# A hybrid decoder layer on one core: four Strassen pieces instead of three in each SwiGLU down product, and two of four weight sums per piece made by adding DMAs

## The chip, the core and the metric

The kernel runs on one NeuronCore of a Trainium2 chip. Five engines work side by side on their own instruction queues: TensorE (PE, matrix products; PEld is its loading of stationary operands), VectorE (DVE), ScalarE (ACT), GpSimd (POOL) and SyncE (SP, which here only issues DMAs). Data lies in DRAM, is brought by DMA into SBUF (128 partitions), and products accumulate in PSUM banks of 128 x 512 float32. The metric is device microseconds of one execution; lower is better. Before the change three runs took 733.73, 734.62 and 734.84 us.

## What is computed

One decoder layer on 256 tokens of width 1024, float32 throughout: a SwiGLU block with half a residual, a mixer (an SSD branch beside differential attention, merged by gates), and a second SwiGLU block, each between RMS norms. The change touches the down product of both SwiGLU blocks only:

```python
def swiglu(x, w_gate, w_up, w_down):
    return (jax.nn.silu(x @ w_gate) * (x @ w_up)) @ w_down
...
h = h + 0.5 * rmsnorm(swiglu(rmsnorm(h, ffn1_pre_g[l]), ffn1_w_gate[l], ffn1_w_up[l], ffn1_w_down[l]),
                      ffn1_post_g[l])
...
h = h + 0.5 * rmsnorm(swiglu(rmsnorm(h, ffn2_pre_g[l]), ffn2_w_gate[l], ffn2_w_up[l], ffn2_w_down[l]),
                      ffn2_post_g[l])
```

The down weight is 2816 x 1024, so the down product is (256 x 2816) times (2816 x 1024).

## The kernel before

**Float32 by three products.** Every float32 operand x is split into hi, x rounded to the PE's fast 32-bit format, and lo = x - hi. A product is hi*hi + lo*hi + hi*lo: three matmuls where one would do. For weights the split is made while the kernel runs: ScalarE casts a piece of weight to hi (L259 for plain chunks, L130 in `Quad.split`), VectorE subtracts to get lo (L262, L135). So each weight passes through ScalarE and VectorE once, in instructions of 128 x 1024.

**Chunks and buffers.** The list `chunks` holds every weight tile in the order of use, 1 MB each. `load_to` (L231 to L239) issues their loads on SP's queue into `RAW_BUFS` = 3 buffers named raw, so that a new load starts when an older chunk has been split. The split parts, the weight sums (wt), the activations of the down product (gh and gl, a hi and a lo tile for every 512 of the 2816 rows) and the larger sums of activations are all 4 KB tiles of one pool, k4, with `K4_BUFS` = 29 slots. A tile takes a slot at its first write and gives it back after its last reader; an instruction whose tile finds no free slot waits, and so does what is behind it on its engine.

**The down product.** It is cut along its 2816 rows in eleven chunks of 256 rows (numbers 0 to 10). `DOWN` (L49) is the plan: p is one plain chunk, q1 is a piece of two chunks (2 and 3), q2 is 4 and 5, q3 is 6 and 7. A plain chunk needs 24 matmuls of 128 x 512. A piece is a 2 x 2 by 2 x 2 block product, done by Winograd's form of Strassen with seven products in place of eight: 42 matmuls in place of 48. Its weights lie in two raw buffers: the first holds quarters 0 and 1 (upper left and right), the second quarters 2 and 3 (lower left and right). Products 1, 2 and 3 use plain quarters 0, 2 and 3; products 5, 6, 7 and 4 use sums, which VectorE makes in `sum_of` (L122), one sum ahead of its use. `FIRST` and `LAST` (L50) are the orders of the seven products in a piece, `LAST` for the last piece. The sums of the activations are made once per piece in `sums_of` (L667 on), when the piece's chunks of activations are ready.

**Order.** Pieces and the plain chunks between them are done in `mm_quads` over both 128-token blocks at once. The last three plain chunks (`TAIL` = 3) are done in `mm_n` block by block, so that the norm of block 0 runs while the PE works on block 1; between the two parts `combine` (L723 to L729) adds the Strassen products up on VectorE, ordered behind the lo part of the last chunk. `take` (L287) hands out the next split weight and first splits ahead by `AHEAD` = 3 chunks, where a product of a piece counts a quarter of a chunk. `give_back` frees a raw buffer as soon as its two quarters have had their last use, and issues the next load into it. Engines other than the PE follow in this part the order that the scheduler gave them when the kernel was built.

**GpSimd** does little: its queue holds the loads of the norm's gains (`load_gain`, L587) and small work.

Of the kernel before, what the change touches and what calls it, by code (L numbers as in the profile page):

```python
# [26 lines left out]
P = 128  # L27
T = 256
# [17 lines left out]
QK_US = 2.4  # L46
GATE_US = 1.75
SSD_US = 1.55
DOWN = {"f1": "q1 p q2 p q3 ppp", "f2": "q1 p q2 p q3 ppp"}  # L49
FIRST, LAST = (1, 2, 3, 5, 7, 6, 4), (1, 6, 7, 2, 5, 3, 4)  # L50
BREAK, STOP = object(), object()

# [2 lines left out]
def tile_hybrid_layer(ctx: ExitStack, tc: tile.TileContext, x, ffn1_pre_g, ffn1_w_gate, ffn1_w_up,  # L55
# [37 lines left out]
    class Quad:  # L93

        PLAIN = {1: 0, 2: 2, 3: 3}
        SUMS = {5: (1, 0), 6: (3, 5), 7: (3, 1), 4: (2, 6)}

        def __init__(self, i, products):  # L100
            self.i, self.sums, self.products = i, {}, products
            self.uses = [[p for p in products if p in (1, 5)], [p for p in products if p in (5, 7)],
                         [p for p in products if p in (2, 4)], [p for p in products if p in (3, 6, 7)]]

        def quarter(self, n, p):

            self.uses[n].remove(p)
            return raws[self.i + n // 2][:, :, (n % 2) * 512:(n % 2 + 1) * 512]

        def give_back(self):  # L110
            for j in range(2):
# [4 lines left out]
        def sum_of(self, p):  # L116

            if p not in self.sums:
                n, m = self.SUMS[p]
                m = self.sum_of(m) if p in (6, 4) else self.quarter(m, p)  # L120
                t = k4([P, 2, 512], f"wt{self.i}{p}")
                nc.vector.tensor_sub(t, self.quarter(n, p), m)  # L122
                self.sums[p] = t
            return self.sums[p]

        def split(self, p):
            load_to(self.i + 2)
            hi = k4([P, 2, 512], f"wqh{self.i}{p}", F32R)
            src = self.quarter(self.PLAIN[p], p) if p in self.PLAIN else self.sum_of(p)
            nc.scalar.copy(hi, src)  # L130
            for later in self.products[self.products.index(p) + 1:][:1]:
                if later in self.SUMS:
                    self.sum_of(later)
            lo = k4([P, 2, 512], f"wql{self.i}{p}", F32R)
            nc.vector.tensor_sub(lo, src, hi.bitcast(F32))  # L135
            self.give_back()
            return lambda kt: hi[:, kt, :], lambda kt: lo[:, kt, :]

    chunks, units = [], []

    def chunk(src, shape):
        units.append((len(chunks), None))
# [11 lines left out]
    def quad(w, k0, products):  # L156

        n = len(units)
        for k in (k0, k0 + 2 * P):
            n_chunk(w, k)  # L160
        del units[n:]
        q = Quad(len(chunks) - 2, products)
        units.extend((q, p) for p in products)


# [65 lines left out]
    def load_to(n):  # L231
        while len(raws) < min(n, len(chunks)):
            i = len(raws)
            src, shape = chunks[i]
            r = sb.tile(shape, F32, tag="raw", name=f"raw{i}", bufs=RAW_BUFS)
            nj = shape[1] // 4 if i == 0 else shape[1] // 2 if i < 4 else shape[1]
            for j in range(0, shape[1], nj):
                nc.sync.dma_start(r[:, j:j + nj, :], src[:, j:j + nj, :])
            raws.append(r)  # L239

    def split_steps(ahead=True):

# [344 lines left out]
        nc.gpsimd.dma_start(pg, v[0].partition_broadcast(P))  # L587
        return pg

    def mm_n(acc, acts, ready, turned, begun=lambda: None, pairs=None, begin=True, taken_all=lambda: None, norms=None,  # L590
             half=lambda b, q: None, quarters=(), tail=None):


# [8 lines left out]
        def one(i, w, parts, late=True, others=True, cs=slice(0, 512), to=None):  # L602
# [3 lines left out]
            for kt in range(2):  # L606
                ah, al = acts[2 * pairs[i] + kt]
                for b, qs in parts:
                    ts = slice(b * P, (b + 1) * P)
                    for x_, w_ in ((ah, wh), (al, wh), (ah, wl)):  # L610
                        if not (late if kt == 1 and w_ is wl else others):
                            continue
                        for q in qs:
                            nc.tensor.matmul(acc[b][q][:, cs] if to is None else to, x_[:, ts],  # L614
                                             w_(kt)[:, halves[q]][:, cs],
                                             start=to is not None and kt == 0 and x_ is ah and w_ is wh or
                                             begin and i == 0 and kt == 0 and x_ is ah and w_ is wh,
                                             stop=i == n - 1 and kt == 1 and w_ is wl)
                if i == 0:
                    begun()  # L620
# [46 lines left out]
    def sums_of(g, even, odd):  # L667
# [3 lines left out]
        v = k4([P, 4, 2, P], f"sv{g}")  # L671
        hi, lo = ((k3 if g < 3 else k4)([P, 3, 2, P], f"s{n}{g}", F32R) for n in "hl")
        more = k2([P, 2, 2, P], f"s4{g}", F32R)
        nc.vector.tensor_tensor(v[:, 0], even[:, :, bs[1]], odd[:, :, bs[1]], ALU.add)
        nc.vector.tensor_sub(v[:, 2], even[:, :, bs[0]], even[:, :, bs[1]])
        nc.vector.tensor_sub(v[:, 1], v[:, 0], even[:, :, bs[0]])
        nc.vector.tensor_sub(v[:, 3], odd[:, :, bs[0]], v[:, 1])
        split(hi, lo, v[:, 0:3])
        split(more[:, 0], more[:, 1], v[:, 3])
        return ([hi[:, i] for i in range(3)] + [more[:, 0]], [lo[:, i] for i in range(3)] + [more[:, 1]])  # L680
# [1 line left out]
    def mm_quads(acts, sums, tag):  # L682
# [40 lines left out]
        def combine():  # L723
# [1 line left out]
            m = add(u2, bank[6], p1)  # L725
            tc.add_manual_dep(m.ins, last_wlo[0].name, order, reason="behind the last chunk's weights")
            add(u3, bank[7], u2)
            add(u4, bank[5], u2)
            add(c4, bank[5], u3)  # L729

        return acc, [[p1, u4], [u3, c4]], combine, [j for kind, j in down[tag][n_quads:]]

# [75 lines left out]
    def ffn(post_v, tag, ready, turned, then, products):  # L808
# [64 lines left out]
        def done(b):  # L873
            norm_end(norms[b], b, 4.0, tag)
            ready(b)

        mm_n(acc, gu, done, turned, pairs=pairs, begin=False,
             taken_all=combine, norms=norms, half=half, quarters=quarters, tail=tail)


# [687 lines left out]
```

## Time and profile before

| | us |
|---|---|
| three runs | 733.73, 734.62, 734.84 |
| span of the profiled execution, first to last instruction | 732.0 |
| median of the runs less that span | 2.6 |
| PE busy | 724.0 (4025 matmuls) |
| VectorE busy | 609.2 |
| ScalarE busy | 475.3 |
| GpSimd busy | 37.0 |
| DMA, mean over the span | 188 GB/s, 137.92 MB |

The page gives the time that each engine had an instruction in work. The time of the profiled execution outside its span isn't on the page; the runs are 1.7 to 2.8 us longer than the span. Views with windows give the same busy times for a stretch of the span, and the timeline lists instructions with start, duration, engine, line and tiles; a bracket behind a row is the idle time before it and what ended it. The first SwiGLU's down product lies at about 130 to 190 us, the second's at 666 to 725 us, and both run the same code.

### The profile page before, as it was taken

How to read it: one execution, taken by the hardware profiler on the slowest of the kernel's cores; microseconds unless marked ns; L12 is line 12 of the kernel's file. 1: busy time of each engine (PE TensorE's matmuls, PEld its weight loads, DVE VectorE, ACT ScalarE, POOL GpSimd, SP SyncE). 2: the span in 40 equal slices, each digit the busy share in tenths (PEclk: the TensorE clock that was granted, in tenths of full speed). 3: DMA queues.
4: the chain of work that ended last, by engine and by line, in shares of the span. 5: the costliest groups of instructions: out<-in, count | busy, mean ns of one | idle time of the engine just before them, and what ended most of it. 6: DMA issues, size and time to landing. Idle time of an engine off the chain costs nothing.

```text
span 732.0 us, 10570 instructions
## 1 busy us (share of the span) xinstructions
PE 724.0 (99%) x4025; PEld 618.4 (84%) x4025; DVE 609.2 (83%) x948; ACT 475.3 (65%) x815; POOL 37.0 (5%) x66
## 2 busy tenths in 40 slices
PE   9999999999999999999999999999999999999996
PEld 7888888888878889999888888888888888888885
DVE  6978787999979999877996997784784878779995
ACT  6656566656867676869965577772663657566562
POOL 2800000000200000000000000000010000000000
PEclk9999999999999999999999999999999999999999
DMA  8874645467673647666564664475471664654541
GB/s 290 241 247 157 225 146 203 173 210 279 182 228 118 201 146 250 187 192 207 159 221 146 215 209 147 140 246 187 129 238 35 231 195 153 227 205 145 185 185 57
DMA packets 94210, 137.92 MB, mean 188 GB/s; under 512 B 2684, under 2 KB 68304, under 8 KB 94160
## 3 DMA queue, kind: packets, MB, share of 16 engines
q1 hardware_dynamic: 91488, 129.51, 53.1%
q0 software_dynamic: 2368, 7.22, 3.2%
q8 instruction: 31, 0.51, 0.3%
q10 hardware_dynamic: 304, 0.53, 0.2%
q14 instruction: 19, 0.16, 0.1%
HBM read 136.17 MB, written 1.08 MB: 188 GB/s over the span
## 4 chain that ended last, share of the span: by engine, by line
PE 99%; DVE 0%; ACT 0%; DVEq 0%; issue 0%; ACTq 0%
PE pup_f L326 9%; PE pg_f L326 9%; PE pws L345 6%; PE pgt L345 6%; PE acc_f1p L692 5%; PE acc_f2p L692 5%; PE pxs L326 4%; PE pg_f L325 4%; PE pup_f L325 4%; PE pn_f L355 3%; PE acc_mx L614 3%; PE pn_mx L345 3%; PE pn_f L345 3%; PE pwd L345 3%; PE acc_f1p L614 2%; PE acc_f2p L614 2%
## 5 line engine op out<-in xcount | busy, mean ns | idle before, releaser
L262 DVE TENSOR_TENSOR wlo<-raw,whi 128x1024 fp32r<-128x1024 f32 (+1 forms) x222 | 262.2, 1209 | 19.5 <-ACT whi L259 18.3
L259 ACT CAST whi<-raw 128x1024 fp32r<-128x1024 f32 (+1 forms) x221 | 222.8, 1043 | 12.8 <-PE psc L1255 2.5
L326 PE MATMUL pup_f<-u_f,whi 128*128 128x512 f32 x288 | 101.5, 396 | 0.0
L326 PE MATMUL pg_f<-u_f,whi 128*128 128x512 f32 x288 | 101.3, 396 | 0.0
L325 PE MATMUL pg_f<-u_f,wlo 128*128 128x256 f32 x252 | 70.6, 280 | 0.0
L325 PE MATMUL pup_f<-u_f,wlo 128*128 128x256 f32 x252 | 70.3, 279 | 0.0
L326 PEld LDWEIGHTS pup_f<-u_f,whi 128*128 128x128 f32 x288 | 52.9, 188 | 9.9
L326 PEld LDWEIGHTS pg_f<-u_f,whi 128*128 128x128 f32 x288 | 52.8, 188 | 9.7
L325 PEld LDWEIGHTS pg_f<-u_f,wlo 128*128 128x128 f32 x252 | 47.5, 189 | 1.7
L325 PEld LDWEIGHTS pup_f<-u_f,wlo 128*128 128x128 f32 x252 | 47.5, 189 | 1.6
L326 PE MATMUL pxs<-u_mx,whi 128*128 128x512 f32 x128 | 44.6, 397 | 0.0
L130 ACT CAST wqh<-wt 128x1024 fp32r<-128x1024 f32 x24 | 25.3, 1054 | 23.3 <-DVE wt L122 22.1
L330 ACT COPY su_f<-pup_f 128x256 f32<-128x256 f32 x36 | 13.4, 372 | 37.5 <-PE pup_f L326 37.4
L331 DVE TENSOR_TENSOR su_f<-pup_f,su_f 128x256 f32<-128x256 f32 x36 | 15.1, 421 | 25.0 <-ACT su_f L330 24.9
L345 PE MATMUL pgt<-whi,u_mx 128*128 128x512 f32 x128 | 33.1, 393 | 0.0
L311 PE MATMUL pz<-u_mx,whi 128*128 128x256 f32 x128 | 31.8, 285 | 0.0
L312 PE MATMUL pz<-u_mx,whi 128*128 128x256 f32 x128 | 31.4, 283 | 0.0
L325 PE MATMUL pxs<-u_mx,wlo 128*128 128x256 f32 x112 | 31.2, 279 | 0.0
L135 DVE TENSOR_TENSOR wql<-wt,wqh 128x1024 fp32r<-128x1024 f32 x24 | 29.2, 1218 | 0.2
L345 PEld LDWEIGHTS pgt<-whi,u_mx 128*128 128x128 f32 x128 | 23.6, 188 | 5.3 <-issue 0.7
L326 PEld LDWEIGHTS pxs<-u_mx,whi 128*128 128x128 f32 x128 | 23.2, 188 | 4.2
L301 ACT CAST gh_f<-sg_f 128x512 fp32r<-128x512 f32 x18 | 11.2, 620 | 23.0 <-DVE sg_f L848 23.0
(415 smaller groups left out, 1699.1 us busy)
## 6 DMA issues: line engine op xcount, KB each, us to landing
raw<-in_w_in_dram SPq DMA_DIRECT2D x40, 1024.0 KB, 5.2
raw<-in_ffn_w_down_dram SPq DMA_DIRECT2D x22, 1024.0 KB, 4.9
raw<-in_ffn_w_gate_dram SPq DMA_DIRECT2D x20, 1024.0 KB, 5.2
raw<-in_ffn_w_up_dram SPq DMA_DIRECT2D x20, 1024.0 KB, 5.2
raw<-in_ssd_w_branch_dram SPq DMA_DIRECT2D x8, 1024.0 KB, 4.9
acb<-acd POOLq DMA_DIRECT2D x8, 512.0 KB, 5.0
raw<-in_da_w_branch_dram SPq DMA_DIRECT2D x4, 1024.0 KB, 4.9
raw<-in_w_out_dram SPq DMA_DIRECT2D x4, 1024.0 KB, 4.9
```

Source lines behind the costliest of these rows:

```text
L130: nc.scalar.copy(hi, src)
L135: nc.vector.tensor_sub(lo, src, hi.bitcast(F32))
L259: behind(copy(hi[:, js, :], r[:, q * nj + j:q * nj + j + n, :]), "cast")
L262: m = nc.vector.tensor_sub(lo[:, js, :], r[:, q * nj + j:q * nj + j + n, :], hi[:, js, :].bitcast(F32))
L311: nc.tensor.matmul(acc[m], wh(j)[:, cs], ah(k0 + j), start=first and j == ks[0], stop=False)
L312: nc.tensor.matmul(acc[m], wh(j)[:, cs], al(k0 + j), start=False, stop=False)
L325: nc.tensor.matmul(acc[:, :T], wl(j)[:, cs], ah(j), start=False, stop=False)
L326: nc.tensor.matmul(acc, wh(j)[:, cs], ahl(j), start=j == 0, stop=j == KD - 1)
L345: nc.tensor.matmul(acc, a(k0 + j), b(j), start=first and i == 0, stop=last and i == 11)
L355: nc.tensor.matmul(accs[b], x_(k0 + j), w_(j), start=first and j == 0 and w_ is wh and x_ is acts[b][0], stop=last and j == 3 and w_ is wl)
L614: nc.tensor.matmul(acc[b][q][:, cs] if to is None else to, x_[:, ts], w_(kt)[:, halves[q]][:, cs], start=to is not None and kt == 0 and x_ ...
L692: nc.tensor.matmul(bank[p], x_, w_, start=p not in begun, stop=last and p in (1, 5, 6, 7))
```

## The change

`DOWN` becomes "q1 q2 q3 q4 ppp" for both blocks: chunks 8 and 9 become a fourth piece, the pieces stand in a row, and the three plain chunks 0, 1 and 10 come last. For each piece two of the four weight sums aren't made by VectorE any more. `added`, called when the piece's first raw buffer is loaded, lets GpSimd's queue add quarter 0 from DRAM into quarter 1 in the raw buffer (product 5's sum, with accumulating DMA), takes a k4 tile, loads quarter 1 into it on SP's queue, and adds quarter 3 to it with a second accumulating DMA on GpSimd's queue (product 7's sum). The sums then are additions with the opposite sign for some, so signs turn in `sum_of`, `sums_of` and `combine`. Quarter 0 is now used by products 1 and 6, quarter 1 by 5, quarter 2 by 2 and 4, quarter 3 by 3. `begin` of `mm_n` becomes a function, since the bank of the fourth block of the result now gets its first product only in the tail.

```diff
--- before.py
+++ after.py
@@ -46,7 +46,7 @@
 QK_US = 2.4
 GATE_US = 1.75
 SSD_US = 1.55
-DOWN = {"f1": "q1 p q2 p q3 ppp", "f2": "q1 p q2 p q3 ppp"}
+DOWN = {"f1": "q1 q2 q3 q4 ppp", "f2": "q1 q2 q3 q4 ppp"}
 FIRST, LAST = (1, 2, 3, 5, 7, 6, 4), (1, 6, 7, 2, 5, 3, 4)
 BREAK, STOP = object(), object()
 
@@ -94,18 +94,27 @@
 
 
 
-        PLAIN = {1: 0, 2: 2, 3: 3}
-        SUMS = {5: (1, 0), 6: (3, 5), 7: (3, 1), 4: (2, 6)}
-
-        def __init__(self, i, products):
-            self.i, self.sums, self.products = i, {}, products
-            self.uses = [[p for p in products if p in (1, 5)], [p for p in products if p in (5, 7)],
-                         [p for p in products if p in (2, 4)], [p for p in products if p in (3, 6, 7)]]
+        PLAIN = {1: 0, 5: 1, 2: 2, 3: 3}
+
+        def __init__(self, i, w, k0, products):
+            self.i, self.w, self.k0, self.sums, self.products = i, w, k0, {}, products
+            self.uses = [[p for p in products if p in (1, 6)], [5], [p for p in products if p in (2, 4)], [3]]
 
         def quarter(self, n, p):
 
             self.uses[n].remove(p)
             return raws[self.i + n // 2][:, :, (n % 2) * 512:(n % 2 + 1) * 512]
+
+        def of_dram(self, k, c):
+            return self.w[self.k0 + k * T:self.k0 + (k + 1) * T, c * 512:(c + 1) * 512].rearrange(
+                "(j p) c -> p j c", p=P)
+
+        def added(self):
+
+            nc.gpsimd.dma_start(raws[self.i][:, :, 512:], self.of_dram(0, 0), accum_op=ALU.add)
+            t = self.sums[7] = k4([P, 2, 512], f"wt{self.i}7")
+            nc.sync.dma_start(t, self.of_dram(0, 1))
+            nc.gpsimd.dma_start(t, self.of_dram(1, 1), accum_op=ALU.add)
 
         def give_back(self):
             for j in range(2):
@@ -116,10 +125,10 @@
         def sum_of(self, p):
 
             if p not in self.sums:
-                n, m = self.SUMS[p]
-                m = self.sum_of(m) if p in (6, 4) else self.quarter(m, p)
+                n, m = {6: (0, 7), 4: (2, 6)}[p]
+                m = self.sum_of(m)
                 t = k4([P, 2, 512], f"wt{self.i}{p}")
-                nc.vector.tensor_sub(t, self.quarter(n, p), m)
+                nc.vector.tensor_tensor(t, self.quarter(n, p), m, ALU.add)
                 self.sums[p] = t
             return self.sums[p]
 
@@ -129,7 +138,7 @@
             src = self.quarter(self.PLAIN[p], p) if p in self.PLAIN else self.sum_of(p)
             nc.scalar.copy(hi, src)
             for later in self.products[self.products.index(p) + 1:][:1]:
-                if later in self.SUMS:
+                if later in (4, 6):
                     self.sum_of(later)
             lo = k4([P, 2, 512], f"wql{self.i}{p}", F32R)
             nc.vector.tensor_sub(lo, src, hi.bitcast(F32))
@@ -138,7 +147,7 @@
 
 
 
-    chunks, units = [], []
+    chunks, units, quads = [], [], {}
 
     def chunk(src, shape):
         units.append((len(chunks), None))
@@ -159,7 +168,7 @@
         for k in (k0, k0 + 2 * P):
             n_chunk(w, k)
         del units[n:]
-        q = Quad(len(chunks) - 2, products)
+        q = quads[len(chunks) - 2] = Quad(len(chunks) - 2, w, k0, products)
         units.extend((q, p) for p in products)
 
 
@@ -237,6 +246,8 @@
             for j in range(0, shape[1], nj):
                 nc.sync.dma_start(r[:, j:j + nj, :], src[:, j:j + nj, :])
             raws.append(r)
+            if i in quads:
+                quads[i].added()
 
     def split_steps(ahead=True):
 
@@ -587,7 +598,7 @@
         nc.gpsimd.dma_start(pg, v[0].partition_broadcast(P))
         return pg
 
-    def mm_n(acc, acts, ready, turned, begun=lambda: None, pairs=None, begin=True, taken_all=lambda: None, norms=None,
+    def mm_n(acc, acts, ready, turned, begun=lambda: None, pairs=None, begin=lambda b, q: True, taken_all=lambda: None, norms=None,
              half=lambda b, q: None, quarters=(), tail=None):
 
 
@@ -614,7 +625,7 @@
                             nc.tensor.matmul(acc[b][q][:, cs] if to is None else to, x_[:, ts],
                                              w_(kt)[:, halves[q]][:, cs],
                                              start=to is not None and kt == 0 and x_ is ah and w_ is wh or
-                                             begin and i == 0 and kt == 0 and x_ is ah and w_ is wh,
+                                             begin(b, q) and i == 0 and kt == 0 and x_ is ah and w_ is wh,
                                              stop=i == n - 1 and kt == 1 and w_ is wl)
                 if i == 0:
                     begun()
@@ -671,10 +682,10 @@
         v = k4([P, 4, 2, P], f"sv{g}")
         hi, lo = ((k3 if g < 3 else k4)([P, 3, 2, P], f"s{n}{g}", F32R) for n in "hl")
         more = k2([P, 2, 2, P], f"s4{g}", F32R)
-        nc.vector.tensor_tensor(v[:, 0], even[:, :, bs[1]], odd[:, :, bs[1]], ALU.add)
+        nc.vector.tensor_sub(v[:, 0], even[:, :, bs[1]], odd[:, :, bs[1]])
         nc.vector.tensor_sub(v[:, 2], even[:, :, bs[0]], even[:, :, bs[1]])
         nc.vector.tensor_sub(v[:, 1], v[:, 0], even[:, :, bs[0]])
-        nc.vector.tensor_sub(v[:, 3], odd[:, :, bs[0]], v[:, 1])
+        nc.vector.tensor_tensor(v[:, 3], odd[:, :, bs[0]], v[:, 1], ALU.add)
         split(hi, lo, v[:, 0:3])
         split(more[:, 0], more[:, 1], v[:, 3])
         return ([hi[:, i] for i in range(3)] + [more[:, 0]], [lo[:, i] for i in range(3)] + [more[:, 1]])
@@ -725,8 +736,8 @@
             m = add(u2, bank[6], p1)
             tc.add_manual_dep(m.ins, last_wlo[0].name, order, reason="behind the last chunk's weights")
             add(u3, bank[7], u2)
-            add(u4, bank[5], u2)
-            add(c4, bank[5], u3)
+            nc.vector.tensor_sub(u4, bank[5], u2)
+            nc.vector.tensor_sub(c4, bank[5], u3)
 
         return acc, [[p1, u4], [u3, c4]], combine, [j for kind, j in down[tag][n_quads:]]
 
@@ -874,7 +885,7 @@
             norm_end(norms[b], b, 4.0, tag)
             ready(b)
 
-        mm_n(acc, gu, done, turned, pairs=pairs, begin=False,
+        mm_n(acc, gu, done, turned, pairs=pairs, begin=lambda b, q: b == q == 1,
              taken_all=combine, norms=norms, half=half, quarters=quarters, tail=tail)
 
 
```

## The prediction

> **What bounds the kernel now.** I read the page first (engine shares), then the chain of waits over the first down product, then windows over its parts, then VectorE's timeline there, and last the DMA issues.
>
> ```profile
> PE 724.0 (99%) x4025; PEld 618.4 (84%) x4025; DVE 609.2 (83%) x948; ACT 475.3 (65%) x815; POOL 37.0 (5%) x66
> ```
>
> The PE is in work nearly all of the span, so a matmul less is time less, if nothing else gets late. The chain in the down product says the same:
>
> ```profile
> 133.63 39.03 PE acc_f1p L692 x172
> 172.66 12.30 PE acc_f1p L614 x54
> 184.96 1.07 PE pu_mx L470 x8
> 186.03 4.12 PE acc_f1p L614 x18
> ```
>
> Start, length, matmuls: three pieces and two plain chunks in one unbroken run at 39.03/172 = 0.227 us a matmul, then the tail. But VectorE is as full there. The windows (core, length, PE, PEld, DVE, ACT, POOL busy, clock, DMA share, GB/s) show the end of the up products, then piece 1, plain, piece 2, plain, piece 3, tail of block 0:
>
> ```profile
> 124.00:128.00 4.00, 4.00 (x25) 3.51 (x24) 4.00 (x5) 2.32 (x4) 0.00 (x0) 1.00 0.00 0
> ...
> 130.20:142.60 12.40, 12.40 (x60) 10.35 (x59) 11.37 (x14) 9.16 (x13) 0.00 (x0) 1.00 0.62 229
> 142.60:148.00 5.40, 5.40 (x25) 4.48 (x24) 5.40 (x6) 2.47 (x3) 0.00 (x0) 1.00 0.10 39
> 148.00:157.50 9.50, 9.50 (x43) 7.88 (x42) 9.46 (x9) 5.52 (x6) 0.00 (x0) 1.00 0.64 221
> 157.50:163.00 5.50, 5.50 (x26) 4.53 (x26) 5.37 (x6) 2.61 (x3) 0.00 (x0) 1.00 0.65 202
> 163.00:172.60 9.60, 9.60 (x44) 7.96 (x43) 9.60 (x9) 7.80 (x9) 0.53 (x1) 1.00 0.58 216
> 172.60:184.90 12.30, 12.30 (x56) 9.96 (x55) 11.93 (x17) 7.84 (x12) 0.00 (x0) 1.00 0.81 302
> ```
>
> VectorE works 53.1 of the last six rows' 54.7 us. How near it is to being the bound is in its timeline (the last two products of piece 3, then the three plain chunks) and in the waits:
>
> ```profile
> 168.28 1.23 DVE L135 TENSOR_TENSOR wql<-wt,wqh 128x1024 fp32r<-128x1024 f32 x1
> 169.42 4.62 DVE L262 TENSOR_TENSOR wlo<-raw,whi 128x1024 fp32r<-128x1024 f32 x4
> 174.31 2.36 DVE L262 TENSOR_TENSOR wlo<-raw,whi 128x1024 fp32r<-128x1024 f32 x2 [0.27 <-ACT whi L259]
> ...
> PEld acc_f1p L614 <- DVE wlo L262: 0.2, 1, 0.2
> ```
>
> Piece 3's last lo is ready at 169.5; its product 4 starts 6 matmuls before 172.66, at 171.3, and reads that lo from its third matmul, at 171.75: 2.2 us in hand. Of the tail's six lo parts the fifth is ready at 174.31 + 1.23 = 175.5, wanted 14 matmuls after 172.66, at 175.8; and the PE has already waited 0.2 us there. So in the tail VectorE's margin is nil: the PE's end of block 0 is VectorE's end too.
>
> **The change, part by part** (each down product; the second repeats the first).
>
> *Matmuls.* A piece has 42, the two plain chunks that it replaces 48: six fewer, 6 x 0.227 = 1.36 us less PE work; both products 2.72 us.
>
> *Weights on VectorE.* All its instructions of 128x1024 follow each other every (4.62 - 1.22)/3 = 1.13 us, by the row at 169.42. Before: three pieces of 7 lo and 4 sums, five plain chunks of 2: 43. After: four pieces of 7 and 2, three plain chunks: 42. That saves 1.13 us.
>
> *Sums of activations.* Piece 4 needs a set of its own; piece 3's stands here:
>
> ```profile
> 101.23 0.42 DVE L674 TENSOR_TENSOR sv<-sg_f,sg_f 128x256 f32<-128x256 f32 x1
> 101.69 0.43 DVE L676 TENSOR_TENSOR sv<-sv,sg_f 128x256 f32<-128x256 f32 x1
> 102.04 0.69 DVE L302 TENSOR_TENSOR gl_f<-sg_f,gh_f 128x512 fp32r<-128x512 f32 x1
> 102.64 0.42 DVE L677 TENSOR_TENSOR sv<-sg_f,sv 128x256 f32<-128x256 f32 x1
> 103.03 0.96 DVE L302 TENSOR_TENSOR sl<-sv,sh 128x768 fp32r<-128x768 f32 x1
> ...
> 105.12 0.42 DVE L302 TENSOR_TENSOR s<-sv,s 128x256 fp32r<-128x256 f32 x1
> 105.46 1.22 DVE L262 TENSOR_TENSOR wlo<-raw,whi 128x1024 fp32r<-128x1024 f32 x1
> ```
>
> From start to next start 0.46 + 0.35 + 0.39 + 0.95 + 0.34, and 0.35 for the fourth sum (it has no row): 2.84 us. They wait for chunk 9's activations, so they fall behind the row at 125.27 below, where VectorE is full. VectorE's work thus grows by 2.84 - 1.13 = 1.71 us where the PE's shrinks by 1.36: a swing of 3.07 us against a margin of nil.
>
> *Idle that could take it up.*
>
> ```profile
> 119.23 1.22 DVE L135 TENSOR_TENSOR wql<-raw,wqh 128x1024 fp32r<-128x1024 f32 x1
> 120.37 0.41 DVE L331 TENSOR_TENSOR su_f<-pup_f,su_f 128x256 f32<-128x256 f32 x1
> 122.66 1.23 DVE L135 TENSOR_TENSOR wql<-raw,wqh 128x1024 fp32r<-128x1024 f32 x1 [1.87 <-ACT wqh L130]
> ...
> 125.27 0.68 DVE L848 TENSOR_TENSOR sg_f<-su_f,sg_f 128x512 f32<-128x512 f32 x1
> ...
> 131.68 1.22 DVE L135 TENSOR_TENSOR wql<-wt,wqh 128x1024 fp32r<-128x1024 f32 x1
> ```
>
> The 1.87 us are a wait for piece 1's second raw buffer. Now product 5 could be split there, since its sum arrives in the first buffer. Between 0 and 1.87 I take 1.3.
>
> *Slots of k4.* At 131.68 VectorE makes product 7's lo. Then five pairs gh, gl (10) and the third piece's sums (2) are held: 17 of 29 slots are left for weights. After the change piece 4's sums (2) and the two tiles loaded ahead for products 7 of pieces 1 and 2 are held too: 13. The last chunk of the up product holds 4 until 133.63, and products 1, 2, 3, 5 with the sum for 6 take 9: product 7's hi has no slot before 133.63; with 1.05 us of cast its lo comes at 134.8, against 131.68 + 2.84 - 2 x 1.13 = 132.3 by work alone. That is up to 2.5 us lost, less what VectorE does out of turn (that up chunk's additions): 0 to 2.5, I take 1.5.
>
> *Raw buffers.*
>
> ```profile
> DMA to landing us min/median/max: 4.7/4.9/6.3
> ```
>
> A load takes 4.9 us. In a row of pieces, a piece's second buffer is loaded when the piece before has made its sum for 6, five VectorE instructions (5.7 us) ahead of its own first use; 4.9 and a cast of 1.05 are 6.0. The tail's second and third chunks hang in the same way on product 5 and product 3 of piece 4. 0.3 us too late at each place, up to 1.7 with 6.3; partly covered by the other stalls, I take 0.4 in all.
>
> *ScalarE* gets 3 more casts and 3 fewer waits for sums; it is busy 7.80 of 9.60 us at most in the rows above, and that covers them. Uncovered they would cost 3 x 1.05.
>
> *Adding DMAs.* No row shows one. The nearest are plain ones of 512 KB from GpSimd's queue, the gain (issued at 168.65, under a full VectorE) first:
>
> ```profile
> 168.65 0.53 POOL L587 DMA_DIRECT2D pg_f<-in_ffn_post_g_dram  x1 [135.22 <-PE acc_f1p L692]
> ...
> DMA to landing us min/median/max: 5.7/5.7/5.7
> ...
> DMA to landing us min/median/max: 4.0/5.0/6.0
> ```
>
> The last row is that of acb. I take 5.7 for an add, bounded by 4.0 and by twice 5.7 = 11.4, if reading the destination costs as much again. It is needed soonest in piece 4, whose order begins 1, 6, 7: its first buffer is issued after piece 2's sum for 4, eleven VectorE instructions or 12.5 us ahead. Load 4.9, the load behind it about 1.4 more, issue 0.53, add 5.7: 12.5. Just in time, cost 0; with 11.4 it is 5.7 us late, once per down product. Bytes: a piece moves 2.10 MB plus three times 0.52, 3.67 MB in nine VectorE instructions (10.2 us), 360 GB/s, below what the tail moves:
>
> ```profile
> 172.00:176.00 4.00, 4.00 (x19) 3.19 (x19) 3.73 (x4) 2.06 (x3) 0.00 (x0) 1.00 1.03 410
> ```
>
> The Trainium skill (DMA: Bandwidth & Descriptors, Anatomy of one DMA) fits a GpSimd-issued transfer as 2.0 us plus bytes over 436 GB/s, an estimate of 3.2 us for 512 KB. The trace's 5.7 is longer and includes the issue. By the page even a doubled add (6.4) would be only 0.7 us late, and the sum would stay as it is. The same page (Rules for kernel authors) says that an accumulate reads its destination and writes it later; no run here shows what this costs.
>
> *Sum.* Stall per down product 3.07 - 1.3 + 1.5 + 0.4 = 3.67 us; less 1.36 saved: +2.31. Twice: +4.6. The profiled execution has 732.0 us of span and, by the runs, about 2.6 us outside it, which nothing here touches; 732.0 + 4.6 + 2.6 = 739.2. The bounds of the terms by themselves: every stall gone, -2.72, 731.9; no reuse of idle, 2.5 of slots and 1.7 of raw, 2 x (7.27 - 1.36) = +11.8, 746.4; adds at 11.4 on top of the sum, 750.6.
>
> **Rivals.**
>
> *VectorE keeps up (faster).* The mechanism: half of the weight sums leave VectorE, and within the pieces it needs nine instructions (10.2 us) to the PE's 42 x 0.227 = 9.53, where it needed 11 before. If its lead at the first product is kept, the 1.7 us of the first buffer's sums are hidden before 130 us, and the three plain chunks behind the row are loaded in time, nothing stalls: 734.62 - 2.72 = 731.9. For it speaks that the casts' waits for sums disappear in part; against it that VectorE is full from 124 us on (4.00 of 4.00 us), ahead of the row. It decides at a stall below 1.36 us per product.
>
> *Even.* Stalls of 0.6 to 2.1 us per product: 733.2 to 736.1.
>
> *The adds are the bound.* Adds of 8 to 12 us, from the second read or from GpSimd's one queue, where the second add stands behind the first; then piece 4's products 6 and 7 are late by 2.5 to 6 us per product on top of the sum: 744 to 751, say 747. Against it: GpSimd's queue is empty there (0.00 in six of the seven windows).
>
> *The pieces do not come in a row*, because SP's queue stands before the tile for product 7: an SP that waits for a k4 slot holds up the raw loads queued behind it. Price as a whole raw load per piece, 4.9 us less the 0.8 to 3 in hand, thus 8 to 16 us per product. By the count above slots are free again after 133.63, and the first two tiles are taken before the squeeze; I give it little.
>
> **How the numbers follow.** Forecast (VectorE late, 736 to 744) 0.50; keeps up 0.18; even 0.12; adds bound 0.15; SP's queue 0.05. A change of less than 0.2%, 1.5 us, could not be told from none. So faster 0.18, same 0.12, slower 0.70. For the range I leave out the far ends: 731.8 to 750; the likeliest case's own is 736 to 744.
>
> **What would show it.** PE matmuls fall by 12 in all, and none of 128 x 512 gets longer. VectorE shows 16 sums at L122's successor, not 24, and six more lo. If I am right, the chain of waits leaves the PE in piece 4 and at the tail's first lo parts, with PE idle before them of 2 to 5 us per down product, released by VectorE's lo, and VectorE has idle near 131 us released by the PE (a slot). If the adds bound it, the idle is before piece 4's sum for 6, released by a DMA. I am wrong if PE idle in both down products together stays below 2.7 us.

## The result and the profile after

The changed kernel takes 768.53 us (median of 4 runs, 765.95 to 772.28) against 734.17 us (733.53 to 734.84) of the kernel before on the same chip: 34.4 us more, a ratio of 1.047 with a 95% interval of 1.0446 to 1.0495. The forecast was slower, 739.2 us, range 731.8 to 750. The direction was right; the loss is more than seven times the predicted 4.6 us and lies outside the range.

From the page of the profiled execution after the change (span 765.6 us, before 732.0), first the engines, then the shares of the chain that ended last:

```profile
PE 735.5 (96%) x4013; PEld 620.9 (81%) x4013; DVE 614.1 (80%) x958; ACT 482.8 (63%) x825; POOL 55.7 (7%) x82
PE 82%; DMA 10%; DVE 4%; ACT 2%; issue 2%; POOL 0%; DVEq 0%; SPq 0%; ACTq 0%
```

The twelve matmuls are gone (4025 to 4013), yet the PE is busy 11.5 us *longer*, so that some matmuls must have become slower. VectorE has 4.9 us more work, where the forecast had 2 x 1.71. Neither explains 34 us. What is new is the 10% of DMA on the chain. In the first down product that chain is (start, length, what):

```profile
134.16 8.47 DMA raw<-in_ffn_w_down_dram
142.72 1.06 ACT wqh L139
...
147.29 1.15 DVE wt L131
...
148.50 8.72 DMA raw<-in_ffn_w_down_dram
...
158.28 2.00 ACT wqh L139 x2
...
160.32 0.83 POOL raw L114
...
161.64 10.12 DMA wt<-in_ffn_w_down_dram
...
171.84 1.24 DVE wt L131
...
181.91 7.82 DMA raw<-in_ffn_w_down_dram
...
192.16 10.43 PE acc_f1p L625 x40
202.59 0.87 PE pu_mx L481 x8
```

Before, this stretch was one run of matmuls and the norm began at 184.96 us; now it begins at 202.59, 17.6 us later, and the second down product loses the rest. The chain is a circle through the raw buffers: the load of a piece's second half takes 8.5 us; ScalarE casts it (L139); VectorE subtracts, and then makes the sum for product 6 (L131), the last use of the piece's first raw buffer; only then does the load of the next piece's second half start, into that buffer. From one such load to the next it takes 148.50 - 134.16 = 14.3 us, while the PE needs 9.5 us for a piece. In the third turn an add of piece 4 stands in the circle too: GpSimd issues the add into the raw buffer (L114) and behind it the one into wt, which takes 10.1 us and holds up piece 4's sum for product 6.

The page's list of DMA issues says the same for all loads (count, KB each, median us from issue to landing):

```profile
raw<-in_ffn_w_down_dram SPq DMA_DIRECT2D x22, 1024.0 KB, 8.8
wt<-in_ffn_w_down_dram SPq DMA_DIRECT2D x8, 512.0 KB, 10.0
raw<-in_ffn_w_down_dram POOLq DMA_DIRECT2D x8, 512.0 KB, 6.2
wt<-in_ffn_w_down_dram POOLq DMA_DIRECT2D x8, 512.0 KB, 10.5
```

Before, the first of these rows had the same 22 loads with 4.9, the load time on which the prediction built. The windows (columns as in the prediction) show why, and what follows from it:

```profile
120.00:170.00 50.00, 45.58 (x205) 36.03 (x203) 38.79 (x44) 27.66 (x35) 7.12 (x6) 0.97 0.94 253
...
155.00:160.00 5.00, 1.87 (x7) 0.95 (x6) 1.60 (x2) 2.67 (x3) 0.00 (x0) 1.00 1.03 392
160.00:165.00 5.00, 5.00 (x16) 3.94 (x15) 5.00 (x5) 2.26 (x3) 2.38 (x2) 0.66 0.68 118
...
170.00:175.00 5.00, 0.72 (x2) 0.63 (x3) 3.10 (x3) 1.82 (x2) 0.00 (x0) 0.90 0.77 296
175.00:180.00 5.00, 5.00 (x19) 3.96 (x18) 4.37 (x5) 3.60 (x5) 0.00 (x0) 0.76 0.02 3
```

The DMA engines are 94% busy over 50 us, at only 253 GB/s; the row of before in the prediction moved 410 GB/s at a share of 1.03. So the adds seem to fill the engines without moving so many bytes; the second experiment below measures it. VectorE is no longer full (38.79 of 50). In two stretches the PE is busy for only 1.87 and 0.72 of 5 us, and behind each of them the granted clock is low (0.66 and 0.76). The PE's timeline behind the second gap (start, duration, instruction, in the bracket the idle before it):

```profile
174.28 0.80 PE L703 MATMUL acc_f1p<-wqh,sh 128*128 128x512 f32 x1 [4.50 <-ACT wqh L139]
174.87 0.63 PE L703 MATMUL acc_f1p<-wql,gh_f 128*128 128x512 f32 x1
175.29 0.63 PE L703 MATMUL acc_f1p<-wqh,gh_f 128*128 128x512 f32 x1
...
177.42 0.40 PE L703 MATMUL acc_f1p<-wqh,sh 128*128 128x512 f32 x1
```

Starts are 0.42 us apart behind the gap and 0.24 us from 177.42 on. Some 3.1 us pass at nearly half the pace, about 1.5 us lost beside the 4.5 us of the gap itself. The Trainium skill (TensorE: Matmul & The Clock Gate, Part 1) says that an array that has idled runs at half clock until it has been busy for about 3.4 us; the trace agrees here, with 3.1 us, but behind a gap of 2.99 us in the first experiment the slow pace lasted over 5 us.

The PE's own waits in the same down product (us in total, times, longest):

```profile
PE acc_f1p L703 <- ACT wqh L139: 7.5, 3, 4.5
PE acc_f1p L625 <- ACT whi L270: 2.4, 1, 2.4
PE acc_f1p L703 <- DVE wql L144: 1.1, 2, 0.6
```

With 0.2 us for a lo part of the tail these are 11.2 us. But a product that ends 17.6 us later with 1.36 us less work has lost 19.0 us. The rest is in the pace of the matmuls. If one adds up, from the PE's timeline, how much later than 0.227 us each start comes behind the one before it, the first product loses about 13 us at starts that follow a wait and about 6 us at other starts, the second about 12 and 6. That makes 37 us, less 2.7 us for the twelve matmuls saved: the 34 us measured. So two thirds of the loss is waiting and one third slow matmuls.

Most of the waits are for ScalarE's casts. Those waited for loads, or, ahead of the longest one (4.50 us), for piece 4's sum, which in turn waited for its add:

```profile
DVE wt L131 <- DMA wt<-in_ffn_w_down_dram: 4.1, 1, 4.1
```

### The profile page after: what moved, and what is told of

It reads as the page before. It is cut to its first block, busy times and chain, and to the rows that moved or that the text cites. A ratio compares the mean times of both kernels' runs of the same rounds, so it can differ in the third digit from the quotient of the medians.

```text
span 765.6 us, 10666 instructions
## 1 busy us (share of the span) xinstructions
PE 735.5 (96%) x4013; PEld 620.9 (81%) x4013; DVE 614.1 (80%) x958; ACT 482.8 (63%) x825; POOL 55.7 (7%) x82
## 4 chain that ended last, share of the span: by engine, by line
PE 82%; DMA 10%; DVE 4%; ACT 2%; issue 2%; POOL 0%; DVEq 0%; SPq 0%; ACTq 0%
PE pg_f L337 8%; PE pup_f L337 8%; DMA raw<-in_ffn_w_down_dram 7%; PE pws L356 6%; PE pgt L356 6%; PE pxs L337 4%; PE pg_f L336 4%; PE pup_f L336 4%; PE pn_f L366 3%; PE acc_mx L625 3%; PE pn_mx L356 3%; PE pn_f L356 3%; PE pwd L356 3%; DMA wt<-in_ffn_w_down_dram 3%; PE pz L322 2%; PE pz L325 2%
## 5 line engine op out<-in xcount | busy, mean ns | idle before, releaser
L273 DVE TENSOR_TENSOR wlo<-raw,whi 128x1024 fp32r<-128x1024 f32 (+1 forms) x214 | 252.9, 1209 | 24.6 <-ACT whi L270 23.4
L270 ACT CAST whi<-raw 128x1024 fp32r<-128x1024 f32 (+1 forms) x213 | 214.9, 1044 | 15.8 <-DMA raw<-in_ffn_w_down_dram 6.7
L144 DVE TENSOR_TENSOR wql<-raw,wqh 128x1024 fp32r<-128x1024 f32 x32 | 38.0, 1220 | 14.7 <-ACT wqh L139 14.6
L139 ACT CAST wqh<-raw 128x1024 fp32r<-128x1024 f32 x32 | 32.3, 1047 | 16.9 <-DMA raw<-in_ffn_w_down_dram 16.9
L139 ACT CAST wqh<-wt 128x1024 fp32r<-128x1024 f32 x24 | 25.0, 1049 | 27.9 <-DVE wt L131 27.6
L114 POOL DMA_DIRECT2D raw<-in_ffn_w_down_dram x8 | 9.7, 1211 | 256.6 <-DMA wt<-in_ffn_w_down_dram 100.6
## 6 DMA issues: line engine op xcount, KB each, us to landing
wt<-in_ffn_w_down_dram POOLq DMA_DIRECT2D x8, 512.0 KB, 10.5
```

What stands on the lines that cost most here:

```text
L270: behind(copy(hi[:, js, :], r[:, q * nj + j:q * nj + j + n, :]), "cast")
L273: m = nc.vector.tensor_sub(lo[:, js, :], r[:, q * nj + j:q * nj + j + n, :], hi[:, js, :].bitcast(F32))
```

## The experiments

Four theories are named in the expectations. In short: **A**, the adding itself costs; **B**, the four pieces in a row and their transfers cost, adding or not; **C**, VectorE's work and its k4 slots cost, as predicted; **D**, which came up after the first runs, three raw buffers are too few for the time that the loads now take. Diffs are against the changed kernel unless it says "before". All ratios are against the kernel before on the same chip (733.6 to 734.1 us).

### The sums by DMA left out

```diff
         def added(self):
-            nc.gpsimd.dma_start(raws[self.i][:, :, 512:], self.of_dram(0, 0), accum_op=ALU.add)
-            t = self.sums[7] = k4([P, 2, 512], f"wt{self.i}7")
-            nc.sync.dma_start(t, self.of_dram(0, 1))
-            nc.gpsimd.dma_start(t, self.of_dram(1, 1), accum_op=ALU.add)
+            self.sums[7] = h[:, :, :512]
```

> The changed kernel without the adding DMAs and without the load into the tile for product 7: product 5 takes quarter 1 as it is, product 7 and the sum for 6 take a tile of h in place of their sum, so two weight sums of each piece are left out of the computation. Theory A (an adding DMA is slow and slows every load beside it: 235 to 300 GB/s at a full DMA share in the changed kernel, loads landing in 8.8 us, not 4.9): all of the loss goes, 731 to 736 us. Theory B (it is the row of four pieces through three raw buffers, whatever fills them): a good part stays, 745 or more. Theory C (the prediction: VectorE's margin is nil, and four pieces give it 1.7 us more to do in each down product): 736 to 740 us, with PE idle of 1.5 to 4 us in each down product behind VectorE's lo.

748.95 us, ratio 1.0202 (1.0185 to 1.0218). So 15 of the 34 us are there without the adds, as B said (745 or more): A alone and C alone are both out. In the trace the first product ends at

```profile
193.49 0.87 PE pu_mx L478 x8
```

8.5 us later than before, and the loss is at the tail (windows, then the matmul behind the gap):

```profile
176.00:180.00 4.00, 1.46 (x4) 0.67 (x4) 1.39 (x2) 0.17 (x1) 0.00 (x0) 0.94 1.03 408
180.00:184.00 4.00, 3.03 (x6) 1.99 (x7) 3.06 (x4) 3.42 (x4) 0.00 (x0) 0.50 0.82 316
```

```profile
180.93 0.79 PE L622 MATMUL acc_f1p<-whi,gh_f 128*128 128x512 f32 x1 [2.99 <-ACT whi L267]
```

All engines are mostly idle at 176 to 180 us while the DMA engines are full. The two loads that the tail waits for were issued at 169.20 and 171.47 us, once piece 4 gave its buffers back, and the next stage's at 174.95 and 177.41. The one of 171.47 took 8.28 us. Before, the loads of the last three chunks went out at 156.66, 161.42 and 168.32. My reading is that a plain chunk between two pieces holds one raw buffer, not two, so that the loads gain a lead while the PE works on it; with the pieces in a row the lead is gone.

### Plain transfers in place of the adds

```diff
-            nc.gpsimd.dma_start(raws[self.i][:, :, 512:], self.of_dram(0, 0), accum_op=ALU.add)
+            nc.gpsimd.dma_start(raws[self.i][:, :, 512:], self.of_dram(0, 0))
...
-            nc.gpsimd.dma_start(t, self.of_dram(1, 1), accum_op=ALU.add)
+            nc.gpsimd.dma_start(t, self.of_dram(1, 1))
```

> The changed kernel with both adding DMAs turned into plain ones of the same bytes, queue, place and waits; they overwrite what they should be added to, so the two sums are left out. Theory A (the adding itself is what costs): 734 to 743 us, loads landing in 5 to 6 us, DMA near 390 GB/s where it is full. Theory B (bytes, waits on GpSimd's queue and three raw buffers): within 5 us of the changed kernel, 762 to 773 us.

755.1 us, 1.0288 (1.0266 to 1.0311), between the two forecasts. The same transfers, waits and queue cost 6.1 us over leaving them out; that they add costs 13.4 more. The rows of GpSimd's queue (packets, MB, share of 16 engines' time) of this kernel, of the kernel before and of the changed one:

```profile
q0 software_dynamic: 4672, 15.61, 7.0%
```

```profile
q0 software_dynamic: 2368, 7.22, 3.2%
```

```profile
q0 software_dynamic: 6720, 15.61, 9.9%
```

16 transfers of 512 KB take (7.0% x 755.2 - 3.2% x 732.0)/16 = 1.84 us of the engines each when plain, (9.9% x 765.6 - 23.4)/16 = 3.27 when adding: 1.8 times as much for the same bytes.

### Four pieces with all sums on VectorE

Before, with the row of four:

```diff
-DOWN = {"f1": "q1 p q2 p q3 ppp", "f2": "q1 p q2 p q3 ppp"}
+DOWN = {"f1": "q1 q2 q3 q4 ppp", "f2": "q1 q2 q3 q4 ppp"}
...
-        mm_n(acc, gu, done, turned, pairs=pairs, begin=False,
+        mm_n(acc, gu, done, turned, pairs=pairs, begin=lambda b, q: b == q == 1,
```

> The kernel before with the new plan alone: four pieces in a row, all four weight sums on VectorE, no adding DMA. VectorE gets 50 instructions of 128x1024 in a down product where it had 43, 7.9 us more, and 2.8 us of activation sums, the PE 1.36 us less. Theory C (margin nil): 9 to 11 us slower per down product, 750 to 757 us, with VectorE full throughout. If VectorE had a margin that the prediction overlooked: 735 to 748 us. Theory A says nothing else than C here; B: more than 757.

760.82 us, 1.0367 (1.0352 to 1.0383). That is above C's 750 to 757, where only B stood (more than 757). Yet VectorE is full through the pieces, as C had it (from 124 to 180 us it is busy 54.51 of 56); one of the windows:

```profile
150.00:160.00 10.00, 8.21 (x34) 6.15 (x34) 9.97 (x10) 5.63 (x7) 0.00 (x0) 1.00 0.57 210
```

VectorE 9.97 of 10 us, PE four fifths, DMA half. C's sum left out the pace: by the same count over the PE's timeline, this kernel loses about 5 us of its first product at matmul starts that no wait precedes. The changed kernel, which takes two sums of each piece from VectorE, is still 7.7 us slower than this one.

### Three pieces with adds

```diff
-DOWN = {"f1": "q1 q2 q3 q4 ppp", "f2": "q1 q2 q3 q4 ppp"}
+DOWN = {"f1": "q1 p q2 p q3 ppp", "f2": "q1 p q2 p q3 ppp"}
...
-        mm_n(acc, gu, done, turned, pairs=pairs, begin=lambda b, q: b == q == 1,
+        mm_n(acc, gu, done, turned, pairs=pairs, begin=lambda b, q: False,
```

> The changed kernel with the old plan: three pieces with a plain chunk after the first and the second, two sums of each piece by adding DMAs. VectorE loses 6 instructions of 128x1024 per down product (6.8 us), the PE's work is as before. Theory A: slower than before all the same, 740 to 757 us, as 12 adds in place of 16 still slow the loads beside them, with more time between. Theory B (the row): 733 to 737 us, no loss with plain chunks between.

752.65 us, 1.0239 (1.0215 to 1.0264), within A's 740 to 757. The adds cost 19 us without the fourth piece. Row and adds each harm the kernel alone; that both do it through the raw buffers is what the next runs test.

### A fourth raw buffer

The same two lines make three kernels: with the sums left out, the changed kernel itself, and the kernel before as a control. All of them give up two k4 slots to make room.

```diff
-K4_BUFS = 29
+K4_BUFS = 27
...
-RAW_BUFS = 3
+RAW_BUFS = 4
```

> The kernel with the two sums left out (748.95 us), with four raw buffers in place of three and 27 k4 slots in place of 29 to make room. Theory D (a raw buffer comes free too late: the next load is issued just in time and lands late when others run beside it, 8.3 us for the tail's last chunk against 4.9 in the kernel before): the PE's idle of 3 us at that chunk and the slow clock behind it go, 735 to 742 us. Theory C (VectorE's margin): no better than 746 us, worse for two slots fewer.

738.34 us, 1.0063 (1.0048 to 1.0078), within D's 735 to 742: 10.6 of the 15 us of the first experiment are gone.

> The changed kernel (768.53 us) with four raw buffers and 27 k4 slots. Theory D (three raw buffers are what turns slow loads into waits): most of the loss goes, 738 to 750 us. Theory A (the adds take the DMA engines' time, share 1.03 to 1.08 in most windows from 120 to 160 us, so that loads are late however early they are issued): 754 to 768 us.

737.41 us, 1.0047 (1.0032 to 1.0062): 31 of the 34 us are gone, with every add in place. D said 738 to 750 and A 754 to 768; the time lies just below D's low end, and A falls: the adds cost that time only where there are three buffers. From the page, first the engines and the DMA row:

```profile
PE 724.6 (99%) x4013; PEld 615.3 (84%) x4013; DVE 613.5 (83%) x958; ACT 482.4 (66%) x825; POOL 56.0 (8%) x82
...
raw<-in_ffn_w_down_dram SPq DMA_DIRECT2D x22, 1024.0 KB, 6.4
```

The chain through the first down product:

```profile
132.93 9.54 PE acc_f1p L703 x42
...
144.85 1.14 DVE wt L131
...
174.83 2.37 DVE wlo L273 x2
177.24 9.38 PE acc_f1p L625 x40
186.62 1.08 PE pu_mx L481 x8
```

The window of 50 us:

```profile
120.00:170.00 50.00, 48.98 (x232) 40.34 (x231) 46.99 (x49) 33.65 (x41) 5.94 (x5) 1.00 0.83 251
```

No DMA is left in these steps of the chain; piece 1 takes 9.54 us for its 42 matmuls, the granted clock is 1.00, and VectorE is nearly full again. From 142.49 to 177.24 us the chain runs through VectorE's lo parts and sums and ScalarE's casts, with 2.35 us of PE at 159.81 between them: that is the bound that the prediction expected. The product ends 1.66 us later than before.

> The kernel before with four raw buffers and 27 k4 slots, the control for the buffers. Theory D (the old plan's loads were in time with three buffers, thanks to the plain chunks between the pieces): within 1 us of before, 733 to 735 us. If the fourth buffer is worth something by itself: below 732.

736.17 us, 1.0032 (1.002 to 1.0045): the control is itself 2.5 us slower, more than expected. It changes buffers and slots together, but one wait, which the kernel before does not have, points at the slots: VectorE waits for one that a matmul gives back.

```profile
DVE wt L122 <- PE pup_f L325: 2.1, 1, 2.1
```

So of the 3.7 us that the changed kernel loses with four buffers, only some 1.2 belong to the change itself, if the slots cost both kernels alike.

### VectorE's load in piece 4 taken away

Without the sums by DMA, and piece 4 reading piece 3's activation sums in place of its own:

```diff
-                    sums[j // 2] = sums_of(j // 2, even, sg)
+                    sums[j // 2] = sums_of(j // 2, even, sg) if j < 8 else sums[3]
```

> The kernel with the two sums left out (748.95 us), and piece 4 takes piece 3's sums of activations in place of its own, so these six instructions of VectorE (2.84 us in each down product) and two k4 tiles are gone; the fourth piece's products 3, 5, 6, 7 are thus computed from other data. Theory C (VectorE's margin, slots): 2 x 2.84 us and part of the slow clock, 738 to 744 us. Theory D (the raw buffers): the loads come as late as before relative to VectorE, but all earlier; not below 745 us if the tail's load alone is the cause.

742.95 us, 1.0115 (1.0082 to 1.0147), 6.0 below the first experiment. It is in C's range, and below the 745 at which the tail's load alone would have stopped. Those sums cost 2 x 2.84 us of VectorE, and here about all of it is felt. My reading is that they delay the casts and sums that free the raw buffers; the two k4 tiles that went with them may have a share.

The same line in the changed kernel with four raw buffers:

> The changed kernel with four raw buffers and 27 k4 slots (737.41 us), and piece 4 takes piece 3's sums of activations, so VectorE's six instructions (2.84 us in each down product) and two k4 tiles are gone; products 3, 5, 6, 7 of piece 4 are thus computed from other data. Theory C (what is left of the loss once the loads are in time is VectorE's work, as the prediction had it): the PE's waits for VectorE's lo parts go and the saved matmuls show, 731.5 to 734 us. If something else than VectorE holds it there: 735.5 us or more.

735.15 us (10 runs), 1.0019 (1.001 to 1.0029), 2.3 below the changed kernel with four buffers, between the two forecasts and 1.2 above C's upper end. So VectorE's extra work is felt in part only (at most 2.3 of 5.7 us; the two k4 tiles that are free again can't be told from it here). What is left, 1.5 us over the kernel before, is less than what the control loses by the two slots fewer.

### The adds measured by themselves

Before, with one plain transfer of 512 KB and three adds into the same k4 tile on GpSimd's queue at the start of the second SwiGLU, where the DMA engines have little to do.

> The kernel before with four more DMAs on GpSimd's queue at the start of the second SwiGLU block, one after another into a tile that nothing reads: a plain one of 512 KB, then three adding ones of the same bytes. It measures an add away from the down product's crowd. Theory A: an add takes at least 1.5 times the plain one from issue to landing, 6.5 us or more against 4 to 5. Theory B (the crowd makes them slow, not the adding): the same 4 to 5.5 us. The kernel's time stays within 2 us of before.

One run, 733.39 us. The four transfers of the tile, from issue to landing, then GpSimd's instructions that issue them (ns: minimum, median, maximum), then its queue on the page:

```profile
DMA to landing us min/median/max: 4.2/5.7/5.8
```

```profile
L1537 POOL DMA_DIRECT2D probe<-in_ffn_w_down_dram x3: 1197/1197/1261, 555.2 to 567.2; - x3
...
L1535 POOL DMA_DIRECT2D probe<-in_ffn_w_down_dram x1: 810/810/810, 550.7 to 550.7; - x1
```

```profile
q0 software_dynamic: 3328, 9.32, 5.0%
```

The 4.2 us are the plain transfer's, 5.7 to 5.8 the adds'. Alone an add lands in the 5.7 us that the prediction took: less than the 6.5 that A wanted, and a little more than B's 5.5, or 1.4 times the plain one. But its engine time is again about double: (5.0% x 731.7 - 23.4 - 1.84)/3 = 3.8 us against 1.84. Latency alone did not show that.

### Piece 4's activation sums on GpSimd

The changed kernel with four raw buffers, and

```diff
+        eng = nc.gpsimd if g == 4 else nc.vector
-        nc.vector.tensor_sub(v[:, 0], even[:, :, bs[1]], odd[:, :, bs[1]])
+        eng.tensor_sub(v[:, 0], even[:, :, bs[1]], odd[:, :, bs[1]])
...
```

with the other three sums and their two lo parts moved in the same way.

> The changed kernel with four raw buffers and 27 k4 slots (737.41 us), and GpSimd makes piece 4's sums of activations and their lo parts, six instructions, in place of VectorE. Theory C (with the loads in time, what is left of the loss is VectorE's work, 2.84 us of it in these six): 732 to 735.5 us, perhaps below the kernel before. If GpSimd's instructions hold VectorE up where both read SBUF, or are too slow for piece 4: 737 us or more.

745.13 us, 1.0159 (1.0137 to 1.018), 7.7 us slower than with the sums on VectorE: C's 732 to 735.5 is missed, and the other branch (737 or more) holds. Two things in the trace fit that; how much each costs was not measured. ScalarE's cast of a sum waits for GpSimd, with the weight casts behind it, and VectorE is slower beside GpSimd. The waits, then the timeline:

```profile
ACT sh L312 <- POOL sv L688: 3.3, 1, 3.3
```

```profile
128.39 1.85 POOL L313 TENSOR_TENSOR sl<-sv,sh 128x768 fp32r<-128x768 f32 x1
129.69 1.63 DVE L144 TENSOR_TENSOR wql<-raw,wqh 128x1024 fp32r<-128x1024 f32 x1 [4.80 <-ACT wqh L139]
```

VectorE was idle 4.80 us for that cast, and its instruction took 1.63 us where 1.22 is usual.

### Three pieces, adds, four raw buffers

The kernel of "Three pieces with adds" with the two lines of the fourth raw buffer.

> Three pieces with plain chunks between and two sums of each piece by adding DMAs (752.65 us), now with four raw buffers and 27 k4 slots. Theory D (with one buffer more the adds are early enough to be hidden): 732 to 736 us. Theory A (the DMA engines' time for the adds is the bound): 743 to 752 us.

732.92 us (10 runs; before 733.63), 0.9991 (0.9981 to 1.0): the fastest of all, not clearly faster than before. Against the control with the same buffers it gains 3.2 us. In its window the loads are slow, median 7.0 us, and the DMA engines nearly full, yet the PE works without a gap:

```profile
132.00:172.60 40.60, 40.60 (x183) 33.68 (x182) 38.30 (x35) 28.78 (x32) 2.94 (x3) 1.00 0.91 272
```

The runs side by side, in us:

| | sums on VectorE | sums by adding DMAs |
|---|---|---|
| three pieces, 3 raw buffers | 734 (before) | 752.7 |
| four pieces, 3 raw buffers | 760.8 | 768.5 (after) |
| three pieces, 4 raw buffers | 736.2 | 732.9 |
| four pieces, 4 raw buffers | not run | 737.4 |

The adds cost 19 and 8 us with three buffers; with three pieces and four buffers they gain 3.

## Why the prediction was wrong

**The failed step is "Raw buffers".** It took a load for a fixed 4.9 us, found the buffers 0.3 us late at a few places and charged 0.4 us per product, 1.7 at most. That 1.7 is the lateness of one place with the slowest load; a row of pieces has several, and each turn starts where the one before ended late. In the changed kernel the median load takes 8.8 us, and the circle of load, cast, sum, and load again through three buffers takes 14.3 and 14.6 us a piece. Even in the run without the adds, where the load issued at 146.98 us landed after 4.8, the next turn began at 157.61, 10.6 us later, against the PE's 9.5. The fourth buffer takes back 31.1 us, 15.6 per product, and without the adds 10.6 us, 5.3 per product, in place of the 0.4 charged; the control shows that it gives the kernel before nothing. The forecast's own count held the warning: a plan that is 0.3 us late at each place with a load of the quiet trace has no room for a load that is 4 us longer.

**"Adding DMAs", cost 0, failed in two ways.** The latency of an add by itself was right (5.7 us taken, 5.7 to 5.8 measured), but the load on the DMA engines was judged by bytes: 360 GB/s against the tail's 410. An add takes 1.8 to 2 times the engine time of a plain transfer, so the engines are full at 253 GB/s and every load and add takes longer. And the forecast's line for piece 4 (load 4.9, load behind it 1.4, issue 0.53, add 5.7: 12.5 us, just in time) came out much longer:

```profile
150.73 0.37 SPq L247 DMA_DIRECT2D raw<-in_ffn_w_down_dram  x1
```

From this issue of piece 4's first buffer to the landing of its add into wt, at 161.64 + 10.12 = 171.76, 21.0 us pass. The rival "The adds are the bound" had the right place and about the right sizes: piece 4's sum for product 6 waits for its add, the sign that the forecast named for it, 4.1 us in the first product and 8.6 in both, and the add into wt takes 10.5 us median against its 8 to 12. It stopped at 751 us because it let the adds delay piece 4 only, and not the loads of every piece.

**The row of pieces** was charged inside "Raw buffers" with the same 0.3 us a place. By the first experiment the first product ends 8.5 us later with it, before any add.

**The clock.** "None of 128 x 512 gets longer" is wrong: behind the gaps matmuls start 0.42 us apart for 3 us and more. The forecast charged a wait at its length; here a wait of 4.5 us costs about 1.5 more, and slow starts make up a third of the whole loss.

**"VectorE late", the forecast's own story, is not what this kernel shows.** In the first product the PE waits 1.3 us for VectorE's lo parts, where 2 to 5 were forecast, and VectorE has no wait for a k4 slot: ScalarE could cast product 7's hi of piece 1 at 131.49 us, where "Slots of k4" (1.5 us) had no slot before 133.63.

**Right:** twelve matmuls fewer; 16 sums on VectorE and six more lo parts (56 instructions for the pieces against 42, eight fewer for plain chunks):

```profile
L144 DVE TENSOR_TENSOR wql<-raw,wqh 128x1024 fp32r<-128x1024 f32 x32 | 38.0, 1220 | 14.7 <-ACT wqh L139 14.6
L144 DVE TENSOR_TENSOR wql<-wt,wqh 128x1024 fp32r<-128x1024 f32 x24 | 29.1, 1221 | 0.3
L131 DVE TENSOR_TENSOR wt<-raw,wt 128x1024 f32<-128x1024 f32 x16 | 19.5, 1219 | 8.6 <-DMA wt<-in_ffn_w_down_dram 8.6
```

Their number is as foreseen; what grew is the idle before them, for casts (14.6 us) and for the adds (8.6 us). VectorE as the bound, with k4 slots as a second cost, comes back once the loads are in time: the changed kernel with four buffers loses 3.7 us, near the predicted 4.6, and 1.66 in the first product against 2.31. That nearness proves little for the terms, since the control loses 2.5 of the 3.7 by itself. "SP's queue", the rival in which SP waits for a slot before the tile for product 7, is seen, but small; this is its one wait for a slot in the first product:

```profile
SPq L116 <- PE acc_f1p L703: 0.7, 1, 0.7
```

What stays open is what four pieces would do with four raw buffers and all 29 k4 slots, which was not run, and how the last 2.3 us of the run with piece 3's sums divide between VectorE's work and the slots.

## What to carry to other kernels

Where a load's buffer is freed just in time, price the whole circle (load, cast, last use, next load) against the work that it feeds, with the load time of a *crowded* stretch, not with the quiet trace's median. Judge DMA work by the engines' busy share, not by GB/s; an add into SBUF takes nearly twice a plain transfer's engine time. Before moving work to DMAs, look for a spare buffer: with three pieces, the adds lost 19 us without one and gained 3 with it.

## What the runs showed of the hardware

An accumulating DMA of 512 KB takes 3.3 to 3.8 us of the 16 engines' time against 1.84 for a plain one, though alone it lands only 1.4 times as late (5.7 against 4.2 us); its issue holds GpSimd for 1.2 us against 0.8. In the changed kernel the PE's granted clock fell to half around waits of 2.4 to 4.5 us. The matmuls were slow for 3.1 us behind the wait of 4.50, and for 6.5 us behind one of 3.89 in the second product (starts 0.43 us apart up to 720.05); in the kernel with the sums left out, behind the gap of 2.99 us, which ended at 180.93 us and had 1.46 us of work in the window of 4 us before, the clock was still 0.50 from 185 to 186 us and 1.00 from 187. VectorE's 128x1024 subtraction took 1.63 us beside GpSimd instructions, 1.22 otherwise. The Trainium skill (SBUF — State Buffer, SBUF: two separate sides) has the two engines contend for a shared port of SBUF, and this row agrees in kind.
